# Moving the low weight buffers 128 bytes against the high ones in a two-block float32 encoder kernel

## The chip, the cores and the metric

The kernel runs on one NeuronCore of a Trainium2 chip. The metric is the device time of one execution in microseconds (us); the number of record is the median of several runs. Beside it there is one profiled execution, whose trace the rows below come from.

## The reference

Two encoder blocks in float32, on a sequence of 256 tokens (272 with 16 meta tokens) of width 1024, each two layers deep. Cut to what matters:

```python
# first block: layer 0 (even) is two attentions side by side, layer 1 (odd) a gated recurrence
zp = einsum('btd,de->bte', rms_norm(h, g), w_in)      # 1024 -> 4288 (even), 4096 (odd)
y = concat([mla_mixer(...), swa_mixer(...)]) * silu(gate)      # even
y = (lru_direction(forward) + lru_direction(reverse)) * silu(gate)   # odd
h = h + einsum('bte,ed->btd', y, w_out)               # 2048 -> 1024
# second block, two layers
for l in range(2):
    x = x + 0.5 * swiglu(rmsnorm(x), w_gate, w_up, w_down)     # ffn1: 1024 -> 2 x 2816 -> 1024
    x = x + hybrid_mixer(rmsnorm(x), ...)                      # pooling and a chunked linear attention
    x = x + 0.5 * swiglu(rmsnorm(x), ...)                      # ffn2
```

Nearly all arithmetic is in these matrix products; the four swiglu layers hold the largest part.

## The kernel before

**Three matmuls for one product.** The products have to keep float32 accuracy, so each operand is held as two parts: a high part (`hi` for weights, names that end in `h` for activations) and a low part, the remainder (`lo`, and names that end in `l`). Each weight piece comes from HBM into a buffer `raw`; ScalarE (ACT) writes `hi` from it and VectorE (DVE) writes `lo = raw - hi` (`cut`). `prod` then issues three matmuls for each block of 128 rows of the contraction: `hi` with the activation's high part, `hi` with its low part, and `lo` with its high part. The weights are the stationary operand (128 columns, 512 bytes of each partition), loaded into TensorE by an LDWEIGHTS that the profile lists as PEld; the activations are the moving operand, of 256 columns in most stages and 272 in the first block:

```python
self.mm(out=out, lhsT=hi if i < 2 else lo, rhs=(xl if i == 1 else xh)[:, k, cols], ...)
```

**What stands where.** Four `hi` and four `lo` buffers of 4096 bytes for each partition lie one after the other in the pool `const` (`make`); a fifth pair is added by `more_cuts` after the even layer. `xh` and `xl` hold the normed activations; for 256 columns they are used through the views `sh` and `sl`, which `place` puts `X_AT` = 32 columns (128 bytes) behind the start of the tiles. `ph` and `pl` hold the hidden layer of a swiglu (22 blocks of 256 columns), `oyh`/`oyl`, `hh`/`hl`, `hph`/`hpl` and `mh`/`ml` the moving operands of the odd and the hybrid layers. `gap` takes some bytes of a pool so that what is allocated next starts later. A block of weights is 512 bytes and a block of 256 columns 1024 bytes, so all blocks of such a tile start at one residue modulo 256.

**Order.** The order of instructions is written by the program itself: `Builder` keeps a clock of assumed costs and lets helper routines run when their inputs are due. The order depends on these costs and on which buffer comes free first, not on addresses.

**Stages in the profile's time.** Even layer to about 309 us, odd layer to 455; then for each of the two layers of the second block: `ffn1` (gate and up products with `xh`/`xl`, then the down products with `ph`/`pl`), the hybrid layer, `ffn2`. The down products run at about 579 to 634, 922 to 992, 1108 to 1170 and 1466 to 1527 us. Counted in the code, one swiglu issues 22 x 2 x 8 x 3 = 1056 matmuls for gate and up and 8 x 22 x 3 = 528 for down.

Of the kernel before, what the change touches and what calls it, by code (L numbers as in the profile page):

```python
# [9 lines left out]
F32 = mybir.dt.float32  # L10
F32R = mybir.dt.float32r
# [5 lines left out]
P = 128  # L17
D = 1024
NM = 16
S = 256  # L20
T = NM + S
KD = D // P
# [40 lines left out]
def weight_plan():  # L63

    out = []

    def add(name, i, n, step=1024):
        out.append((name, i, [(a, min(a + step, n)) for a in range(0, n, step)]))

    for c in range(2):  # L70
        add("first", c, 2048)
    for c in range(2, 8):
        add("ein", c, 2048)
    add("evs", 0, 2048)
    for c in range(12, 16):
        add("ein", c, 2048)
    for c in range(3):
        add("uq", c, 1536, 768)
    for c in range(2):
        add("ukv", c, 2048)  # L80
    for c in range(8, 12):
        add("ein", c, 2048)
    for d in range(KD):
        add("eout", d, 2048)
    for kind, g in odd_order():
        if kind == "w":
            add("oout", g, 2048)
        else:
            for c in range(2):
                add("oin", 2 * g + c + 8 * (kind == "g"), 2048)  # L90
    for l in range(2):
        for f in ("ffn1", "ffn2"):
            for e in range(KFF):
                add(f + "_gu", l * KFF + e, 2048)
            for d in range(2 * KD):
                add(f + "_dn", l * 2 * KD + d, DFF // 2, 768)
            if f == "ffn1":
                for c in range(4):
                    add("hin", l * 16 + c, 2048)
                for c in range(2):  # L100
                    add("hi", l * 2 + c, 2048)
                for c in HYBRID:
                    add("hin", l * 16 + c, 2048)
                for c in range(4):
                    add("wph", l * 4 + c, 2048)
                for c in range(4):
                    add("hout", l * 4 + c, 2048)
    return out
# [11 lines left out]
class Clock:  # L120
# [4 lines left out]
    def __init__(self):  # L125
        self.at = dict.fromkeys(("pe", "act", "dve", "pool", "dma", "dma2"), 0.0)
        self.wrote, self.read = {}, {}
        self.mark, self.tables, self.banks = 0.0, (), set()

    def range(self, ap):  # L130
        dims = list(ap.ap)
        per = dims[0][0] or 1 << 30
        lo = ap.offset % per
        return ap.tensor.name, lo, lo + 1 + sum((n - 1) * abs(s) for s, n in dims[1:])
# [92 lines left out]
class Builder:  # L227

    AHEAD = 3
    X_AT = 32  # L230
    gaps = 0

    def __init__(self, ctx, tc, a):
        self.clock = Clock()
        self.ctx, self.tc, self.nc, self.a = ctx, tc, Core(tc.nc, self.clock), a
        nc = self.nc
        self.tt, self.ts, self.stt, self.ttr = nc.vector.tensor_tensor, nc.vector.tensor_scalar, nc.vector.scalar_tensor_tensor, nc.vector.tensor_tensor_reduce
        self.act, self.mm = nc.scalar.activation, nc.tensor.matmul
        self.cos, self.done, self.cur, self.lists, self.home, self.stalls = [], {}, None, {}, {}, 0
        self.loads = weight_plan()  # L240
        self.plan = [(n, i, ps, p) for n, i, ps in self.loads for p in range(len(ps))]
        self.load_at = self.conv_at = self.use_at = 0
        self.raws, self.conv = [], {}
        self.const = self.pool(ctx, "const")
        self.res = self.pool(ctx, "res", 2)
        psum = self.pool(ctx, "psum", space=PSUM)
        self.make(psum, "acc", 2, [P, 512])
        self.make(psum, "m", 6, [P, 512])
        self.make(self.const, "raw", 2, [P, 2048])
        self.make(self.const, "hi", 4, [P, 1024], F32R)  # L250
        self.make(self.const, "lo", 4, [P, 1024], F32R)
        self.make(self.const, "work", 8, [P, T + 4])
        self.make(self.const, "mx", 6, [P, 16])
# [9 lines left out]

    def gap(self, pool, n):

        if n:
            self.gaps += 1
            pool.tile([P, n // 4], F32, tag=f"gap{self.gaps}", name=f"gap{self.gaps}")

    def make(self, pool, name, n, shape, dt=F32):  # L270

# [221 lines left out]

    def feed(self, gen, d, x, g, n):
        if n == S:
            self.place(gen)
            self.split(x, self.sh[:, d, :], self.sl[:, d, :], g)
        else:
            self.split(x, self.xh[:, d, :n], self.xl[:, d, :n], g)
        self.put("x", gen, d)  # L500
        self.spawn(self.square(gen, d, x, n))

    def place(self, gen):

        at = self.X_AT
        self.sh, self.sl = [t.rearrange("p k t -> p (k t)")[:, at:at + KD * S].rearrange("p (k t) -> p k t", t=S) for t in (self.xh, self.xl)]

    def square(self, gen, d, x, n):
        yield from self.idle("act")
# [591 lines left out]
    def odd(self):  # L1101
# [5 lines left out]
        od = self.pool(st, "od")  # L1107
# [9 lines left out]
        n = 32  # L1117
        at = V_AT["lam"][0]
# [6 lines left out]
        def decay_rates():  # L1125
# [20 lines left out]
            ts(out=c8[:, 1, :], in0=r(5), scalar1=-8.0, scalar2=None, op0=ALU.mult)  # L1146
            self.put("c8")

        yh = [self.t(od, [P, G, S], f"oyh{i}", F32R) for i in range(2)]
        yl = [self.t(od, [P, G, S], f"oyl{i}", F32R) for i in range(2)]  # L1150
        xcs, zgs = {}, {}
# [277 lines left out]
    def more_cuts(self):  # L1429

        late = self.pool(self.ctx, "late")
        for n in ("hi", "lo"):
            self.lists[n].append(self.t(late, [P, 1024], n + "4", F32R))
        self.AHEAD = 4
        self.lbw = self.t(late, [P, 10, 4], "lbw")
        self.hyb = self.t(late, [P, H_N], "hyb")
        self.nc.sync.dma_start(out=self.hyb, in_=self.a["hyb"])
# [33 lines left out]
    def hybrid(self, layer, gen):  # L1471
# [5 lines left out]
        st = ExitStack()  # L1477
        self.phase(gen)
        hy = self.pool(st, "hy")
        self.gap(hy, 32)  # L1480
        self.make(hy, "kq", 2, [P, H, S])
        x, xh, xl = self.x, self.sh, self.sl
        cols = slice(0, S)
# [260 lines left out]
        for c in HYBRID:  # L1744
            e = 2 * c
            if e < 12:
                dst, name, e0 = up_, "u", 8
            elif e < 16:
                dst, name, e0 = og, "g", 12
                self.need("og free", gen)  # L1750
            else:
                dst, name, e0 = gz, "z", 16
# [257 lines left out]
```

## Time and profile before

| | |
|---|---|
| median of 3 runs | 1540.03 us (1538.16 to 1541.54) |
| profiled execution, its own time | 1542.62 us |
| its span, first to last instruction | 1540.5 us |
| TensorE (PE) busy | 1507.8 us, 98%, 12950 matmuls |
| weight loads (PEld) busy | 1473.7 us, 96% |
| DVE busy, ACT busy | 1115.9 us (72%), 904.9 us (59%) |
| mean granted TensorE clock | 0.996 |

How to read it: matmuls are pipelined, one starts before the one ahead of it has ended, so the busy share says that TensorE is always at work, but not how fast. The pace is read from the time between the starts of two matmuls, or from how many of them a stretch holds. A matmul's record lasts about 0.28 us, so a count over a stretch takes in some 2.4 that began before it.

### The profile page before, as it was taken

Reading aid. Unit: us, or ns where it says so; the run is one execution under the profiler, and the core shown is the slowest. Engines: PE = TensorE matmul, PEld = TensorE weight load, DVE = VectorE, ACT = ScalarE, POOL = GpSimd, SP = SyncE. Lnnn points to the kernel's source line nnn. Section 1 sums busy time; section 2 is a strip of 40 time slices with the busy share of each in tenths; the row PEclk is TensorE's granted clock in tenths of the full one; section 3 lists DMA queues with packets and bytes.
Section 4 is the critical chain, followed back from the end, with each engine's and each line's share of the span. In section 5 each row is a group of like instructions: output and inputs, shape, how many; then the busy total and the mean of one; then the engine's idle time right before and its main releaser. Section 6 shows DMA issues by size and latency. Waiting matters only on the chain.

```text
span 1540.5 us, 31049 instructions
## 1 busy us (share of the span) xinstructions
PE 1507.8 (98%) x12950; PEld 1473.7 (96%) x12950; DVE 1115.9 (72%) x1882; ACT 904.9 (59%) x1435; POOL 26.2 (2%) x68
## 2 busy tenths in 40 slices
PE   8999999999989999999999999999999998999998
PEld 8989899999989999989999999999999998999998
DVE  6977775689996666668886666666666787777754
ACT  7666654699966545475455544455455754555453
POOL 1000000000000000000000000000000000000000
PEclk9999999999999999999999999999999999999999
DMA  6422224554445645644355555556456433456553
GB/s 240 152 90 83 84 81 164 182 174 143 156 174 189 218 167 183 211 161 165 137 195 189 196 177 174 194 194 214 161 188 209 167 138 137 163 189 222 175 174 117
DMA packets 42492, 259.12 MB, mean 168 GB/s; under 512 B 4840, under 2 KB 6256, under 8 KB 18416
## 3 DMA queue, kind: packets, MB, share of 16 engines
q1 hardware_dynamic: 40624, 251.90, 47.1%
q10 hardware_dynamic: 1728, 5.24, 1.0%
q8 instruction: 101, 1.65, 0.4%
q14 instruction: 39, 0.32, 0.1%
HBM read 256.07 MB, written 1.05 MB: 167 GB/s over the span
## 4 chain that ended last, share of the span: by engine, by line
PE 63%; issue 19%; DVE 10%; ACT 5%; DMA 2%; POOL 0%; POOLq 0%; ACTq 0%; SPq 0%; DVEq 0%
PE acc L181 51%; PE m L181 12%; DVE lo L181 4%; DVE big L181 3%; ACT hi L181 2%; DMA raw<-in_hin_dram 1%; ACT L181 1%; DVE kq L181 1%; ACT big L181 1%; ACT w L181 0%; DVE xc L181 0%; ACT xx L181 0%; DVE xx L181 0%; DMA raw<-in_ffn_gu_dram 0%; DVE work L181 0%
## 5 line engine op out<-in xcount | busy, mean ns | idle before, releaser
L181 DVE TENSOR_TENSOR lo<-raw,hi 128x1024 fp32r<-128x1024 f32 (+3 forms) x520 | 582.7, 1129 | 258.5 <-ACT hi L181 254.8
L181 ACT ACTIVATE hi<-raw 128x1024 fp32r<-128x1024 f32 (+3 forms) x520 | 502.2, 980 | 297.0 <-PE acc L181 207.8
L181 PE MATMUL acc<-xh,hi 128*128 128x256 f32 (+1 forms) x2096 | 589.7, 281 | 5.4 <-ACT hi L181 5.4
L181 PE MATMUL acc<-xl,hi 128*128 128x256 f32 (+1 forms) x2096 | 590.5, 282 | 0.0
L181 PE MATMUL acc<-xh,lo 128*128 128x256 f32 (+1 forms) x2096 | 588.7, 281 | 0.1
L181 PEld LDWEIGHTS acc<-xh,hi 128*128 128x128 f32 x2096 | 394.5, 188 | 6.8 <-ACT hi L181 5.4
L181 PEld LDWEIGHTS acc<-xl,hi 128*128 128x128 f32 x2096 | 395.6, 189 | 1.4
L181 PEld LDWEIGHTS acc<-xh,lo 128*128 128x128 f32 x2096 | 394.6, 188 | 1.6 <-DVE lo L181 0.5
L181 PE MATMUL acc<-pl,hi 128*128 128x256 f32 x704 | 196.9, 280 | 0.0
L181 PE MATMUL acc<-ph,lo 128*128 128x256 f32 x704 | 196.6, 279 | 0.0
L181 PE MATMUL acc<-ph,hi 128*128 128x256 f32 x704 | 196.4, 279 | 0.0
L181 PEld LDWEIGHTS acc<-pl,hi 128*128 128x128 f32 x704 | 132.2, 188 | 0.0
L181 PEld LDWEIGHTS acc<-ph,hi 128*128 128x128 f32 x704 | 132.2, 188 | 0.0
L181 PEld LDWEIGHTS acc<-ph,lo 128*128 128x128 f32 x704 | 131.8, 187 | 0.0
L181 PE MATMUL m<-xh,lo 128*128 128x256 f32 (+1 forms) x336 | 96.0, 286 | 0.0
L181 PE MATMUL m<-xl,hi 128*128 128x256 f32 (+1 forms) x336 | 95.6, 284 | 0.0
L181 PE MATMUL m<-xh,hi 128*128 128x256 f32 (+1 forms) x336 | 95.5, 284 | 0.0
L181 DVE TENSOR_TENSOR work<-acc,spread 128x256 f32<-128x256 f32 (+1 forms) x108 | 46.0, 426 | 38.0 <-PE acc L181 35.3
L181 ACT ACTIVATE work<-work 128x256 f32<-128x256 f32 (+2 forms) x92 | 37.4, 408 | 51.9 <-DVE work L181 51.5
L181 PEld LDWEIGHTS m<-xh,lo 128*128 128x128 f32 x336 | 63.6, 189 | 0.3
L181 PEld LDWEIGHTS m<-xh,hi 128*128 128x128 f32 x336 | 63.6, 189 | 0.2
L181 PEld LDWEIGHTS m<-xl,hi 128*128 128x128 f32 x336 | 63.5, 189 | 0.1
(359 smaller groups left out, 2242.4 us busy)
## 6 DMA issues: line engine op xcount, KB each, us to landing
raw<-in_ffn_gu_dram SPq DMA_DIRECT2D x88, 1024.0 KB, 4.9
raw<-in_ffn_dn_dram SPq DMA_DIRECT2D x64, 704.0 KB, 4.1
raw<-in_hin_dram SPq DMA_DIRECT2D x32, 1024.0 KB, 4.9
raw<-in_oin_dram SPq DMA_DIRECT2D x16, 1024.0 KB, 5.0
raw<-in_ein_dram SPq DMA_DIRECT2D x12, 1024.0 KB, 4.7
raw<-in_eout_dram SPq DMA_DIRECT2D x8, 1024.0 KB, 4.9
raw<-in_oout_dram SPq DMA_DIRECT2D x8, 1024.0 KB, 4.9
raw<-in_wph_dram SPq DMA_DIRECT2D x8, 1024.0 KB, 4.9
```

What stands on the lines that cost most here:

```text
L181: r = f(*args, **kw)
```

## The change

No instruction is added, removed or moved: on each of the five engines the built program has the same instructions with the same operands in the same order as before. What changes is the address at which tiles start. In the built programs, in bytes modulo 256:

| tile | before | after |
|---|---|---|
| `hi0` to `hi4` | 128 | 128 |
| `lo0` to `lo4` | 128 | 0 |
| `sh`, `sl` (`xh`, `xl` for 256 columns) | 64 | 64 |
| `ph`, `pl` | 192 | 64 |
| `oyh`, `oyl`, `hh`, `hl`, `hph`, `hpl`, `mh`, `ml` | 64 | 64 |
| `xh`, `xl` for 272 columns, block k | 192 + 64 k | 64 + 64 k |

`sh` and `sl` keep the very addresses they had: the tiles start 128 bytes later and the offset of 32 columns inside them is gone. `ff` keeps its gap of 160, so `ph` and `pl` shift with what lies below them.

```diff
@@ class Builder @@
     AHEAD = 3
-    X_AT = 32
     gaps = 0
...
         self.make(self.const, "hi", 4, [P, 1024], F32R)
+        self.gap(self.const, 128)
         self.make(self.const, "lo", 4, [P, 1024], F32R)
...
-    def place(self, gen):
-
-        at = self.X_AT
-        self.sh, self.sl = [t.rearrange("p k t -> p (k t)")[:, at:at + KD * S].rearrange("p (k t) -> p k t", t=S) for t in (self.xh, self.xl)]
+    def place(self):
+
+        self.sh, self.sl = [t.rearrange("p k t -> p (k t)")[:, :KD * S].rearrange("p (k t) -> p k t", t=S) for t in (self.xh, self.xl)]
...
@@ odd @@
+        self.gap(od, 128)
         yh = [self.t(od, [P, G, S], f"oyh{i}", F32R) for i in range(2)]
...
@@ more_cuts @@
-        for n in ("hi", "lo"):
-            self.lists[n].append(self.t(late, [P, 1024], n + "4", F32R))
+        self.gap(late, 128)
+        self.lists["hi"].append(self.t(late, [P, 1024], "hi4", F32R))
+        self.gap(late, 128)
+        self.lists["lo"].append(self.t(late, [P, 1024], "lo4", F32R))
...
@@ hybrid @@
-        self.gap(hy, 32)
+        self.gap(hy, 160)
         self.make(hy, "kq", 2, [P, H, S])
```

## Rows read from the trace of the kernel before

**Rows 1.** The page: busy time by engine, and the granted TensorE clock by slice.
```profile
PE 1507.8 (98%) x12950; PEld 1473.7 (96%) x12950; DVE 1115.9 (72%) x1882; ACT 904.9 (59%) x1435; POOL 26.2 (2%) x68
...
PEclk9999999999999999999999999999999999999999
```
**Rows 2.** What TensorE waited for, the longest total: us, times, longest.
```profile
PE m L181 <- DVE kq L181: 6.4, 12, 0.9
```
**Rows 3.** TensorE groups by form: shape, count, busy us, mean ns, idle before.
```profile
L181 PE MATMUL acc<-xl,hi 128*128 128x256 f32 x1816 | 506.0, 279 | 0.0
...
L181 PE MATMUL acc<-pl,hi 128*128 128x256 f32 x704 | 196.9, 280 | 0.0
...
L181 PE MATMUL acc<-xl,hi 128*128 128x272 f32 x280 | 84.4, 302 | 0.0
...
L181 PE MATMUL m<-xl,hi 128*128 128x256 f32 x232 | 64.7, 279 | 0.0
```
**Rows 4.** Busy time by stretch of the span, all engines.
```profile
core 0: us, PE busy (x) PEld busy (x) DVE busy (x) ACT busy (x) POOL busy (x), PEclk, DMA share, GB/s
470.00:570.00 100.00, 100.00 (x885) 100.00 (x884) 70.75 (x117) 62.39 (x89) 0.00 (x0) 1.00 0.57 201
...
812.00:918.00 106.00, 105.23 (x892) 104.83 (x891) 69.86 (x105) 55.13 (x80) 1.61 (x1) 1.00 0.53 186
...
1000.00:1104.00 104.00, 104.00 (x920) 104.00 (x919) 69.11 (x100) 55.39 (x81) 0.00 (x0) 1.00 0.56 193
...
1304.00:1345.00 41.00, 41.00 (x342) 41.00 (x342) 29.85 (x56) 21.48 (x35) 0.00 (x0) 0.97 0.41 139
...
580.00:634.00 54.00, 54.00 (x461) 54.00 (x460) 34.48 (x55) 26.22 (x40) 0.00 (x0) 1.00 0.55 183
929.00:991.00 62.00, 62.00 (x529) 62.00 (x528) 39.27 (x61) 31.76 (x48) 0.00 (x0) 1.00 0.55 187
```
**Rows 5.** TensorE groups by form, 475 to 565 us, then 812 to 912 us.
```profile
L181 PE MATMUL acc<-xl,hi 128*128 128x256 f32 x248 | 68.4, 276 | 0.0
...
L181 PE MATMUL acc<-xl,hi 128*128 128x256 f32 x256 | 72.1, 282 | 0.0
```
**Rows 6.** Timeline where `ffn1` goes from gate/up to down: start, length (us).
```profile
578.36 0.28 PE L181 MATMUL acc<-xh,hi 128*128 128x256 f32 x1
...
578.70 0.28 PE L181 MATMUL acc<-ph,hi 128*128 128x256 f32 x1
...
579.05 0.28 PE L181 MATMUL acc<-ph,hi 128*128 128x256 f32 x1
...
579.41 0.28 PE L181 MATMUL acc<-ph,hi 128*128 128x256 f32 x1
```
**Rows 7.** Timeline where `ffn2` down ends and the next `ffn1` begins.
```profile
991.54 0.28 PE L181 MATMUL acc<-ph,hi 128*128 128x256 f32 x1
...
991.90 0.28 PE L181 MATMUL acc<-xh,hi 128*128 128x256 f32 x1
...
992.25 0.28 PE L181 MATMUL acc<-xh,hi 128*128 128x256 f32 x1
```
**Rows 8.** Timeline of the odd layer's gate products, first and last of 13.
```profile
344.71 0.28 PE L181 MATMUL m<-xh,hi 128*128 128x256 f32 x1
...
346.12 0.28 PE L181 MATMUL m<-xh,hi 128*128 128x256 f32 x1
```
**Rows 9.** Timeline of a matmul, and of the weight load that starts with it.
```profile
499.94 0.28 PE L181 MATMUL m<-xl,hi 128*128 128x256 f32 x1
...
499.94 0.19 PEld L181 LDWEIGHTS m<-xh,lo 128*128 128x128 f32 x1
```
**Rows 10.** VectorE groups, the costliest: the making of `lo`.
```profile
L181 DVE TENSOR_TENSOR lo<-raw,hi 128x1024 fp32r<-128x1024 f32 (+3 forms) x520 | 582.7, 1129 | 258.5 <-ACT hi L181 254.8 <-PE acc L181 1.5 <-PE m L181 1.4
```

More of the change, by code (lines that the diff above doesn't have):

```diff
@@ L264, in gap @@
     def gap(self, pool, n):
-        if n:
-            self.gaps += 1
-            pool.tile([P, n // 4], F32, tag=f"gap{self.gaps}", name=f"gap{self.gaps}")
+        self.gaps += 1
+        pool.tile([P, n // 4], F32, tag=f"gap{self.gaps}", name=f"gap{self.gaps}")
     def make(self, pool, name, n, shape, dt=F32):
@@ L495, in feed @@
         if n == S:
-            self.place(gen)
+            self.place()
             self.split(x, self.sh[:, d, :], self.sl[:, d, :], g)
```

## The prediction

> **What bounds the kernel now.** I read the page first: TensorE is busy 98% of the span, at the full granted clock in every slice [rows 1]. The waits come next, to see whether another engine holds it up: the longest total is 6.4 us [rows 2], so speeding up or slowing down DVE, ACT or the DMA queues by a little ends nowhere. The time is the number of matmuls times the time from one start to the next, and the change can act on that spacing alone, since it moves no instruction. The groups show that three shapes of three matmuls (high-high, high-low, low-high) carry the kernel, 256 columns each, 1816, 704 and 232 times for each of the three, and that 272 columns come to far less [rows 3]. With the smaller groups there are some 9360 matmuls of 256 columns.
>
> The stretches then give the spacing. From 470 to 570 us TensorE starts 885 matmuls less the 2.4 that lap in: 100 us / 882.6 = 113.3 ns. The same stage one layer on gives 104 / 917.6 = 113.3 ns. From 812 to 918 us, the same program text on `ffn2`, it is 105.2 / 889.6 = 118.3 ns, a little high because eight small matmuls are among them. The two stretches of down products give 54 / 458.6 = 117.7 and 62 / 526.6 = 117.7 ns, and the end of the second hybrid layer 41 / 339.6 = 120.7, where the count also pays for a short stretch at the lower clock [rows 4]. So there are two spacings, 113.3 and close to 117.8 ns; call them fast and slow; the record of one matmul shows them as well, 276 ns against 282 [rows 5]. No wait stands behind the slow one: idle before these groups is 0.0.
>
> Where do they change? At the turn from gate/up to down the start-to-start time of three goes from 0.34 us to 0.35 and 0.36 at once [rows 6]: the moving operand goes from residue 64 to 192 there, the weights staying at 128. The four down stages are all slow. In the other direction, from `ph` back to `xh`, three matmuls still take 0.35 us [rows 7]. So with the moving operand at 64 both spacings can last for a whole stage, and which one it is depends on what came before; at 192 only the slow one is seen. A third piece: in the odd layer's gate products the moving operand of 256 columns goes 0, 64, 128, 192 from one block to the next, and twelve matmuls take 1.41 us, 117.5 ns each, with no fast stretch in between [rows 8]. The weights for a matmul are loaded while the one ahead of it runs: the load of a `lo` block begins with the matmul that uses `xl` [rows 9]. What decides is then, as far as these rows go, where the weights being loaded start against the moving operand being read: 128 - 64 = +64 bytes allows the fast spacing, 128 - 192 = -64 does not.
>
> [...]
>
> **The change, part by part.**
>
> *Low weights at 0.* After the change two loads of three (`hi`) stand at 128 - 64 = +64 against the moving operand and one (`lo`) at 0 - 64 = -64, everywhere. The lower bound of the cost: only the matmul under which `lo` is loaded becomes slow, (2 x 113.3 + 117.8) / 3 = 114.8 ns. The upper bound: a relation that changes within each three leaves no fast stretch at all, as in the gate products, 117.8 ns. I take a value two thirds of the way up, 114.8 + 2/3 x 3.0 = 116.8 ns, because the rows nearest to it (a relation that changes all the time) are slow throughout, and because one step with -64 was enough to end a fast stretch at the turn to `ph`.
>
> *Whom it touches.* Fast before: gate and up of both `ffn1` and of the last `ffn2`, 3 x 1056 = 3168; the end of the first hybrid layer, 384. Slow: gate and up of the first `ffn2`, 1056; the end of the second hybrid layer, 384; the down products, 4 x 528 = 2112. That leaves some 2260 in the odd layer and in the two hybrid layers, where both spacings occur; I halve them. So 4680 fast, 2570 slow at 64 and 2112 slow at 192; the mean is 115.5 ns.
>
> *Moving operands at one residue.* `sh` and `sl` stay where they are, and `oyh`, `hh`, `hph` and `mh` keep their residue: nothing. `ph` and `pl` go from -64 to the mixed relation of all others and so take its 116.8 ns.
>
> *The sum.* 4680 x (116.8 - 113.3) = +16.4 us; 2570 x (116.8 - 117.8) = -2.6; 2112 x (116.8 - 117.7) = -1.9. Together +11.9 us.
>
> *272 columns.* The residues of the moving operand only start at another place of the same circle of four; `lo` changes its relation in one load of three. Spacing is 126 ns or so there and depends on the block; a third of the difference found above, 1.5 ns, over some 1600 matmuls bounds it at 2.4 us either way. I take 0, between them.
>
> *VectorE, ScalarE, DMA.* The writes of `lo` go to other addresses; one takes 1129 ns on DVE, which is busy 71 of 100 us in the fastest stage [rows 4, 10]. Even if it slowed by a tenth, it would lie behind TensorE. The gaps themselves cost a few hundred bytes of SBUF and no instruction. Cost nothing.
>
> The profiled execution took 1542.6 us, span 1540.5, and is 2.6 above the median. 1542.6 + 11.9 = 1554.5 for such an execution, and 1540.0 + 11.9 = **1552 us** for the median.
>
> **The rivals.** All by the new spacing s of 256 columns, each as a mean over the stages; the sign turns at s = 115.5 ns, the mean before.
>
> - *All slow:* s = 117.8. 4680 x 4.5 = +21 us: 1561. For it: the gate products, and the slow stretch that lasts from `ph` into `xh`. Against it: two loads of three keep +64.
> - *Each load by itself:* s = 114.8 everywhere. +7.0 - 7.7 - 6.1 = -7 us: 1533. For it: that is what "the relation of this load decides" would say. Against it: at +64 the slow spacing also lasts, for 106 us at a time.
> - *Fast everywhere (the other side):* a low weight half a period away breaks up the slow order, which then cannot last, and the three find a steady order at 113.3. It saves 2570 x 4.5 + 2112 x 4.4 = 21 us: 1519. For it: both orders are kept up by history, so a shift can just as well remove the slow one; `ph` comes to 64. Against it: no row with a relation that changes is fast.
> - *Nothing:* s stays as it is stage by stage, history decides alone: 1540. Against it: the down products are slow in all four stages.
>
> **How the numbers follow.** Chances: slow with a part kept (my forecast) 0.32, all slow 0.20, nothing 0.13, each load by itself 0.13, fast everywhere 0.22. Faster by over 0.2% (about what a measurement of this kernel can tell from no change) is the sum of the last two, 0.35; slower 0.52; within it 0.13. The likeliest case alone reaches from 1545 to 1559. Since both signs hold much, the range goes from fast everywhere less the bound of the 272 columns, 1517, to all slow plus the same, 1563.
>
> **What would show it.** The same stretches of the profile after: gate and up of `ffn1` at 276 ns and 113.3 ns before should come out near 280 ns and 116 to 118, in every layer alike and without stages of two kinds; the down products between 115 and 118. If the down products come out at 113.3 and no stage at 117.8, the step from "the relation of `lo` is that of `ph`" to "so it is slow" is wrong. If `ffn1` stays fast, one load of three does not break the order. DVE and DMA rows should not move. A spacing below 113.3 anywhere would mean that what I take for the fast order is itself a partly blocked one, and the gain could then pass my range.

## The result: 12 us faster, where 12 us slower was forecast

The changed kernel took 1529.33 us (median of 5 runs, 1526.28 to 1529.65) against 1541.54 us (median of 5 runs of the kernel before on the same chip, 1538.16 to 1546.21). The ratio is 0.991, 95% interval 0.989 to 0.994. The time lies inside the forecast range, but on the other side of no change: the range took in every rival, so that it held the result is no merit of the forecast; to being faster the prediction gave 0.35. The profiled execution of the changed kernel took 1526.28 us, 16.3 us less than the one that [rows 1 to 10] come from.

The page of the changed kernel, busy time by engine and the granted clock, answers to [rows 1]. TensorE issues the same 12950 matmuls in 15 us less; the other engines and the clock did not move.

```profile
PE 1492.8 (98%) x12950; PEld 1458.6 (96%) x12950; DVE 1116.3 (73%) x1882; ACT 903.1 (59%) x1435; POOL 26.2 (2%) x68
...
PEclk9999999999999999999999999999999999999999
```

TensorE groups of the changed kernel by form (shape, count, busy us, mean ns, idle before) answer to [rows 3]: the down products with `pl` went from 280 to 276 ns for one record, and 276 was the mark of the fast spacing in [rows 5]. The 272-column group did not gain.

```profile
L181 PE MATMUL acc<-xl,hi 128*128 128x256 f32 x1816 | 504.3, 278 | 0.0
...
L181 PE MATMUL acc<-pl,hi 128*128 128x256 f32 x704 | 194.3, 276 | 0.0
...
L181 PE MATMUL acc<-xl,hi 128*128 128x272 f32 x280 | 84.7, 303 | 0.0
```

Stretches of the changed kernel, columns as in [rows 4]: gate and up of the first `ffn1`, its down products, gate and up of the first `ffn2`, its down products, and the end of the second hybrid layer.

```profile
470.00:570.00 100.00, 100.00 (x885) 100.00 (x884) 70.34 (x117) 62.65 (x88) 0.00 (x0) 1.00 0.57 198
580.00:630.00 50.00, 50.00 (x444) 50.00 (x443) 33.41 (x52) 25.53 (x41) 0.00 (x0) 1.00 0.56 183
810.00:916.00 106.00, 105.77 (x934) 105.57 (x933) 71.73 (x106) 57.22 (x83) 1.61 (x1) 1.00 0.55 193
926.00:984.00 58.00, 58.00 (x515) 58.00 (x514) 37.58 (x58) 29.32 (x44) 0.00 (x0) 1.00 0.57 194
...
1292.00:1333.00 41.00, 41.00 (x354) 41.00 (x354) 30.45 (x58) 23.08 (x36) 0.00 (x0) 0.97 0.43 147
```

Less the 2.4 that lap in, that is 100/882.6 = 113.3 ns, 50/441.6 = 113.2, 105.77/931.6 = 113.5, 58/512.6 = 113.1, and 41/351.6 = 116.6. The first stretch was fast before and stayed so; the other four were at 117.7 to 120.7 [rows 4]. At the turn from gate/up to `ph`, where three matmuls went from 0.34 to 0.35 and 0.36 us [rows 6], nothing happens now: three take 0.34 us, and the first two with `ph` 0.23 (timeline: start, length):

```profile
578.65 0.28 PE L181 MATMUL acc<-xh,hi 128*128 128x256 f32 x1
...
578.99 0.28 PE L181 MATMUL acc<-xh,hi 128*128 128x256 f32 x1
...
579.33 0.28 PE L181 MATMUL acc<-ph,hi 128*128 128x256 f32 x1
...
579.56 0.28 PE L181 MATMUL acc<-ph,lo 128*128 128x256 f32 x1
```

I also took the starts of the same-numbered matmuls in both traces, stage by stage. Before, the four down stages begin at 578.7, 929.7, 1112.8 and 1469.7 us and last 62.07 us each from first to last start; now each lasts 59.73. That is 2.34 us less for each, 9.4 together; gate and up of the first `ffn2` lost 5.1, the second hybrid layer 2.0, and every other stage, the two layers of the first block among them, moved by 0.5 us or less. All stages together come to 16.2 us, beside 16.3 between the two profiled executions: the gain lies in stages that were slow and became fast, and no stage that was fast became slow. What is still slow is mainly the odd layer's gate products, one record of 281 ns in the changed kernel (group by form, 345.5 to 347.5 us):

```profile
L181 PE MATMUL m<-xl,hi 128*128 128x256 f32 x6 | 1.7, 281 | 0.0
```

One thing in the trace before refines what the prediction read from it. Gate and up of the first `ffn2` did not start slow: 8/70.6 = 113.3 ns up to 812.5 us, after a hybrid layer that had ended fast, and 98/831.6 = 117.8 from 820 us on (columns as in [rows 4]).

```profile
804.50:812.50 8.00, 8.00 (x73) 8.00 (x72) 4.99 (x7) 2.95 (x5) 0.00 (x0) 1.00 0.64 245
...
820.00:918.00 98.00, 98.00 (x834) 98.00 (x834) 64.70 (x95) 52.17 (x77) 0.00 (x0) 1.00 0.55 197
```

Between the two TensorE waited once and issued four small matmuls; three matmuls took 0.33 us ahead of them and 0.35 behind:

```profile
812.70 0.28 PE L181 MATMUL m<-xh,hi 128*128 128x256 f32 x1
...
813.03 0.28 PE L181 MATMUL acc<-xh,hi 128*128 128x256 f32 x1
814.00 0.61 PE L181 MATMUL m<-cst,acc 128*128 128x1 f32 x4 [0.69 <-DVE acc L181]
...
814.79 0.28 PE L181 MATMUL m<-xh,hi 128*128 128x256 f32 x1
...
815.14 0.28 PE L181 MATMUL m<-xh,hi 128*128 128x256 f32 x1
```

The other way round, the second `ffn1` took over the slow spacing from the down products ahead of it and became fast behind four small matmuls at 1000.23 us: three took 0.35 to 0.36 us ahead of them and 0.34 from 1000.92 us on. So "what came before" is not only the stage ahead: at these two places the spacing switched at a short interruption, once in each direction. In the changed kernel the same small matmuls are issued, and behind them the spacing is 113.3 ns again (36 steps from 812.24 to 816.32 us).

### The profile page after: what moved, and what is told of

Read it like the earlier page. It is cut to its first block, busy times and chain, and to the rows that moved or that the text cites. A ratio compares the mean times of both kernels' runs of the same rounds, so it can differ in the third digit from the quotient of the medians.

```text
span 1524.5 us, 31049 instructions
## 1 busy us (share of the span) xinstructions
PE 1492.8 (98%) x12950; PEld 1458.6 (96%) x12950; DVE 1116.3 (73%) x1882; ACT 903.1 (59%) x1435; POOL 26.2 (2%) x68
## 4 chain that ended last, share of the span: by engine, by line
PE 60%; issue 26%; DVE 8%; ACT 4%; DMA 1%; POOL 1%; SPq 0%; ACTq 0%; DVEq 0%; POOLq 0%
PE acc L181 45%; PE m L181 14%; DVE lo L181 3%; ACT hi L181 2%; DVE big L181 2%; DVE kq L181 1%; ACT w L181 1%; ACT L181 1%; ACT xx L181 1%; DVE xx L181 0%; DVE lf L181 0%; DVE work L181 0%; DMA raw<-in_hin_dram 0%; DMA raw<-in_hi_dram 0%; POOL col L181 0%
## 5 line engine op out<-in xcount | busy, mean ns | idle before, releaser
L181 DVE TENSOR_TENSOR lo<-raw,hi 128x1024 fp32r<-128x1024 f32 (+3 forms) x520 | 582.6, 1129 | 248.0 <-ACT hi L181 243.6
```

The lines of the kernel that those rows point to most:

```text
L181: r = f(*args, **kw)
```

## The experiments

Three kernels take the change apart in the model, timed beside the kernel before (1541.64 us, 24 runs, 1536.42 to 1546.14). Two kernels leave the model out and time the threes of matmuls alone, with all other engines idle in the stretches read; each of the two ran once.

### lo_only: the low weights alone

```diff
         self.make(self.const, "hi", 4, [P, 1024], F32R)
+        self.gap(self.const, 128)
         self.make(self.const, "lo", 4, [P, 1024], F32R)
+        self.gap(self.const, 128)
...
-        for n in ("hi", "lo"):
-            self.lists[n].append(self.t(late, [P, 1024], n + "4", F32R))
+        self.lists["hi"].append(self.t(late, [P, 1024], "hi4", F32R))
+        self.gap(late, 128)
+        self.lists["lo"].append(self.t(late, [P, 1024], "lo4", F32R))
+        self.gap(late, 128)
```

The second gap of each pair leaves all that follows at its residue of before (`X_AT` stays 32). Expected:

> The low weights alone go to residue 0; ph stays at 192, everything else at its residue of before. Theory A (weights half a period of 256 bytes apart break up the slow order, wherever the moving operand stands): all stages of 256 columns at 113.3 ns, the down products at ph = 192 too, as in the changed kernel, about 1529 us. Theory B (a moving operand 64 bytes below the high weights is needed as well): the down products stay at 117.8 ns, which is 2112 x 4.5 ns = 9.5 us more than the changed kernel, about 1539 us; gate and up of the first ffn2 become fast.

Measured 1538.29 us (12 runs, 1536.41 to 1541.39), ratio 0.998 (0.997 to 1.000). The same stretches in its trace: first `ffn1`, its down products, first `ffn2`.

```profile
470.00:570.00 100.00, 100.00 (x884) 100.00 (x884) 70.30 (x118) 62.35 (x89) 0.00 (x0) 1.00 0.59 202
580.00:630.00 50.00, 50.00 (x423) 50.00 (x423) 31.46 (x50) 25.05 (x39) 0.00 (x0) 1.00 0.54 175
812.00:916.00 104.00, 102.56 (x902) 102.16 (x901) 71.20 (x107) 55.95 (x81) 1.61 (x1) 1.00 0.55 190
```

Gate and up of `ffn2` became fast, 102.56/899.6 = 114.0 ns with its small matmuls in it. The down products, `ph` at 192, stayed slow, and at 50/420.6 = 118.9 ns a little slower than before. Theory A falls; B stands here: with `lo` at 0 the stages with the moving operand at 64 are fast and those at 192 are not.

### ph_only: the hidden layer alone

```diff
-        self.gap(ff, 160)
+        self.gap(ff, 32)
```

> ph and pl alone go from residue 192 to 64; low and high weights both stay at 128. Theory A (the weights' distance decides): with equal residues both orders can last, so the down products go on with whatever spacing the gate and up products ended with; gate and up of the first ffn2 stay at 117.8 ns. Between 1532 us (three down stages of four fast, 3 x 528 x 4.5 ns = 7 us) and 1541 us. Theory B (the moving operand's residue decides): all four down stages at 113.3 ns and 9.5 us less than before, about 1531 us.

Measured 1537.15 us (12 runs, 1529.47 to 1542.69), ratio 0.997 (0.996 to 0.999). Down products of the first `ffn1`, gate and up of the first `ffn2`, its down products:

```profile
580.00:630.00 50.00, 50.00 (x444) 50.00 (x443) 33.44 (x52) 25.30 (x41) 0.00 (x0) 1.00 0.55 181
812.00:916.00 104.00, 102.94 (x872) 102.54 (x871) 68.54 (x102) 54.00 (x78) 1.61 (x1) 1.00 0.55 190
930.00:988.00 58.00, 58.00 (x495) 58.00 (x494) 37.09 (x59) 29.47 (x45) 0.00 (x0) 1.00 0.57 192
```

The first down stage goes on fast at 113.2 ns after a fast gate/up stage; in `ffn2` gate and up run at 118.4 and its down products at 58/492.6 = 117.7, though nothing about their addresses differs. By the starts of their matmuls three of the four down stages became fast; the third holds 443 from 1110 to 1160 us, 50/440.6 = 113.5 ns. So with both weights at 128 and the moving operand at 64 both orders last, as A says of this set; the residue of `ph` alone does not settle it, and B in its pure form falls. The times tell the same: 13.2 us between fastest and slowest of 12 runs, against 5.0 us in the 12 of `lo_only` and 3.4 us in the 5 of the changed kernel. By itself `lo` brings 3.4 us in the medians and `ph` 4.5; the changed kernel, which has both, brings 12.2, more than their sum.

### swap: the residues of hi and lo exchanged

The changed kernel with `hi` at 0 and `lo` at 128, the rest where it was.

```diff
+        self.gap(self.const, 128)
         self.make(self.const, "hi", 4, [P, 1024], F32R)
         self.gap(self.const, 128)
         self.make(self.const, "lo", 4, [P, 1024], F32R)
+        self.gap(self.const, 128)
...
-        self.gap(late, 128)
         self.lists["hi"].append(self.t(late, [P, 1024], "hi4", F32R))
         self.gap(late, 128)
         self.lists["lo"].append(self.t(late, [P, 1024], "lo4", F32R))
+        self.gap(late, 128)
```

> The changed kernel with the residues of the two weights exchanged: hi at 0, lo at 128, so that two loads of three stand 64 bytes below the moving operand and one 64 above. Theory A (only the distance between the weights counts): no stage slow, about 1529 us. Theory C (two loads of three at +64 are what keeps the fast order): the slow order wins everywhere, 4439 - 558 = 3881 steps of 117.8 instead of 113.3 ns back and the rest too, 1545 to 1561 us.

Measured 1551.79 us (7 runs, 1543.69 to 1557.70), ratio 1.007 (1.004 to 1.009) against the kernel before. First `ffn1` and its down products, then the second `ffn1` and its down products:

```profile
475.00:575.00 100.00, 100.00 (x844) 100.00 (x843) 66.20 (x110) 59.16 (x83) 0.00 (x0) 1.00 0.56 194
586.00:636.00 50.00, 50.00 (x423) 50.00 (x422) 31.46 (x50) 25.08 (x39) 0.00 (x0) 1.00 0.53 178
...
1010.00:1110.00 100.00, 100.00 (x884) 100.00 (x884) 67.31 (x96) 53.52 (x78) 0.00 (x0) 1.00 0.57 197
1122.00:1172.00 50.00, 50.00 (x444) 50.00 (x443) 32.26 (x50) 25.02 (x40) 0.00 (x0) 1.00 0.55 181
```

100/841.6 = 118.8 and 50/420.6 = 118.9 ns, then 113.4 and 113.2 for the same text one layer on. The distance between the weights is that of the changed kernel, so A falls once more. C is right that which weight stands above the moving operand matters, but not that the slow order wins everywhere: this set of residues is two-valued too, with 118.9 in place of 117.8 as its slow value.

### micro: a table of residues

For `hi` at 128, the weights `lo` and the moving operand at four residues each. `hc` is `hi`; `la`, `lb`, `lc`, `ld` stand at 0, 64, 128, 192, and so do `xa` to `xd` (high part of the moving operand) and `ya` to `yd` (low part). The loop, shortened (the pauses are copies on ScalarE):

```python
for l in "cdab":
    for r in "abcd":
        triples(fresh, l, r, 80)      # after a pause
        triples(lead, "c", "d", 32)   # lo at 128, moving at 192
        triples(after, l, r, 80)
```

In the built program the first eight matmuls of `after` mostly stand ahead of the lead, which waits; the rest (232 of 240 in 11 of the 16 cells) follow the lead without a gap, the first lead ending at 49.61 + 11.58 = 61.19 us and they beginning at 61.19, and they are what is read below.

> A kernel of its own that leaves the model out: for each of four residues of the low weights (128, 192, 0, 64; the high weights at 128) and four of the moving operand (0, 64, 128, 192) it issues 80 threes of matmuls of 256 columns twice: once after a pause (fresh), once straight after 32 threes with low weights at 128 and moving operand at 192 (lead, then after). Theory A: low weights at 128: slow order 117.8 ns at moving 192 always, and at 64 after the lead, fast at 64 after a pause; low weights at 0: 113.3 ns in all eight cells of fresh and after. Theory B: low weights at 0 fast only at moving 64. Theory C does not forbid A or B here. Low weights at 192 and 64, a quarter of the period, have no row yet: A as it stands gives between 113.3 and 117.8.

Stretches of 20 us inside five cells: `lo` 128 with moving 64, fresh and after; `lo` 0 with moving 64, fresh and after; `lo` 0 with moving 192, fresh. There is no DVE column, since it does nothing, and no DMA to speak of.

```profile
core 0: us, PE busy (x) PEld busy (x) ACT busy (x) POOL busy (x), PEclk, DMA share, GB/s
92.00:112.00 20.00, 20.00 (x179) 20.00 (x178) 0.00 (x0) 0.00 (x0) 1.00 0.00 1
132.00:152.00 20.00, 20.00 (x172) 20.00 (x172) 0.00 (x0) 0.00 (x0) 1.00 0.01 2
...
650.00:670.00 20.00, 20.00 (x179) 20.00 (x178) 0.00 (x0) 0.00 (x0) 1.00 0.01 2
690.00:710.00 20.00, 20.00 (x179) 20.00 (x178) 0.00 (x0) 0.00 (x0) 1.00 0.01 2
...
788.00:808.00 20.00, 20.00 (x170) 20.00 (x169) 0.00 (x0) 0.00 (x0) 1.00 0.00 1
```

20/176.6 = 113.3 and 20/169.6 = 117.9 for one and the same set; 113.3 and 113.3; 119.3 (one matmul more or less in the count is 0.7). More closely, from the starts of the last 61 matmuls of each cell (their distance / 60), in ns, one number where fresh and after agree to 0.1:

| | moving 0 | moving 64 | moving 128 | moving 192 |
|---|---|---|---|---|
| `lo` 128 | 118.7 | 113.3 fresh, 117.8 after | 120.0 | 117.8 |
| `lo` 192 | 120.0 | 118.2 | 117.8 | 117.8 |
| `lo` 0 | 118.3 | **113.3** | 119.1 | 118.9 |
| `lo` 64 | 120.0 fresh, 117.8 after | 117.8 | 117.8 | 115.6 |

One cell of sixteen is fast both times, `lo` 0 with moving 64: of its run after the lead, the first seven gaps behind the lead are 115 to 122 ns, and then the fast order stands. It is the one into which the change puts all operands of 256 columns outside the odd layer's gate products. The kernel before had its two kinds of stages in the first row: the two-valued cell for moving 64, and a cell that is slow in every reading for `ph`. `lo_only` moves `ph` to the last cell of the third row, 118.9, which its trace shows; B as it stood in the expectation describes the row of `lo` at 0 in this run. Two readings do not show that a cell has one value only: `micro2` has 113.3 for `lo` 0 with moving 192. For the cell of the change more readings speak: its runs and leads in `micro2` and the stages of 256 columns in the changed kernel.

### micro2: pairing, order, 272 columns, and the other lead

```python
CELLS = [(hxl("hc", l, r, r), 272, SLOW) for l in ("lc", "la") for r in "abcd"]
CELLS += [(hxl("hc", l, r, q), 256, SLOW) for l in ("lc", "la") for r, q in ("bd", "db")]
CELLS += [(hxh("hc", "l" + l, r, r), 256, SLOW) for l, r in ("cb", "ab", "ad")]
CELLS += [(hxl("hc", l, r, r), 256, SLOW) for l in ("lc", "la") for r in ("ab", "bc")]
CELLS += [(hxl("hc", "lc", "b", "b"), 256, FAST), (hxl("hc", "la", "d", "d"), 256, FAST), (hxl("la", "lc", "b", "b"), 256, FAST)]
```

`hxl` is the kernel's order, `hxh` issues the two products with the high activations first; `SLOW` is the lead of `micro`, `FAST` is `lo` 0 with moving 64. The two letters in quotes are the high and the low part's tile; `xab` and `xbc` stand at 32 and 96.

> Again threes of matmuls without the model, hi at 128: 50 threes fresh, then 24 threes of a lead, then the same 50 after. Theory P (what counts is, for each load, where the weights being loaded stand against the moving operand read at that moment): with lo left at 128 and only the low activations moved to 192 (xh at 64), the load of lo stands at -64 and the other two at +64, as in the changed kernel, so 113.3 ns fresh and after the slow lead; with lo at 0, xh at 64 and xl at 192 all loads stand at +64, so 113.3 fresh and 117.8 after, as in the kernel before; the order hi-high, lo-high, hi-low at lo 0, moving 64 gives 113.3 in both. Theory Q (the addresses of the two weights against each other count, not the pairing in time): the first of these stays two-valued (113.3 fresh, 117.8 after) and the second is 113.3 in both. After a fast lead: lo 128, moving 64 stays 113.3; lo 0, moving 192 is 118.9 if no fast order exists there and 113.3 if one does; hi 0, lo 128, moving 64 must read the same as the last one if relations alone count. 272 columns at one residue in all blocks: 272/256 x 113.3 = 120.4 ns where 256 columns are fast, 125 or more elsewhere. Moving operands at 32 and 96: between 113.3 and 120.0, no theory says which.

Stretches of 13 us: `lo` 128 with the high part at 64 and the low part at 192, fresh; `lo` 0 with both at 192, fresh, and after the fast lead; `hi` 0, `lo` 128, both at 64, fresh, and after the fast lead; `hxh` with `lo` 0 and moving 64, after the slow lead; 272 columns, `lo` 128, moving 64, fresh.

```profile
416.00:429.00 13.00, 13.00 (x113) 13.00 (x112) 0.00 (x0) 0.00 (x0) 1.00 0.01 1
...
969.00:982.00 13.00, 13.00 (x117) 13.00 (x116) 0.00 (x0) 0.00 (x0) 1.00 0.00 1
996.00:1009.00 13.00, 13.00 (x112) 13.00 (x111) 0.00 (x0) 0.00 (x0) 1.00 0.00 1
1015.00:1028.00 13.00, 13.00 (x111) 13.00 (x111) 0.00 (x0) 0.00 (x0) 1.00 0.01 1
1042.00:1055.00 13.00, 13.00 (x117) 13.00 (x116) 0.00 (x0) 0.00 (x0) 1.00 0.00 1
...
676.00:689.00 13.00, 13.00 (x117) 13.00 (x116) 0.00 (x0) 0.00 (x0) 1.00 0.00 1
...
77.00:90.00 13.00, 13.00 (x108) 13.00 (x107) 0.00 (x0) 0.00 (x0) 1.00 0.01 1
```

A count of 117 is 13/114.6 = 113.4 ns, 111 to 113 are 119.7 to 117.5. By starts 60 apart:

- High part at 64, low part at 192, `lo` 128: 117.8 fresh and after. Theory P falls: load by load the distances are those of the changed kernel (+64, -64, +64), and it is slow. With `lo` 0 the same pair gives 120.9, where both P and Q have 113.3 fresh. Theory Q, which had the first of these two-valued and the second at 113.3 both times, falls too. High at 192, low at 64: 117.8 everywhere.
- `lo` 0 with moving 192 is two-valued: 113.3 fresh here (118.9 fresh in `micro`), 118.9 after either lead. `hi` 0, `lo` 128, moving 64, which has the same distances modulo 256: 118.9 fresh, 113.3 after the fast lead. That is the set of `swap`, and it shows its two kinds of stages without the model. The two sets have the same two values, but after one and the same fast lead the first reads 118.9 and the second 113.3; they were to read the same if distances alone count. For sets with two values that leaves it open. What a pause leaves is open too: the run ahead of the fresh one with `lo` 0, moving 192 was slow in `micro` (119.1) and fast in `micro2` (113.3).
- After the fast lead `lo` 128 with moving 64 stays at 113.3, after the slow one it takes 117.8.
- The order `hxh` changes nothing at moving 64: `lo` 128 is two-valued, `lo` 0 at 113.3 both times.
- Moving operands at 32 and 96: 117.3 to 118.4. In none of the eight readings does the fast spacing show, 32 bytes away from the residue that has it.
- 272 columns: 123.3 at `lo` 128, moving 64; 124.4 to 126.7 in the seven others. No cell reaches 120.4.

No kernel of these beats the changed one. Giving the odd layer's gate products one residue as well would need rows of 320 columns, 3 KB more of each partition for `xh` and `xl` together; it wasn't tried.

## Why the prediction was wrong, point by point

- *What bounds the kernel* was right: TensorE's spacing, and nothing else. The result came from the spacing alone; VectorE's `lo` writes took 1129 ns before and after, so "cost nothing" held for them. That the clock was full "in every slice" is read a little too far, a 9 on the page standing for 90% or more: the end of the second hybrid layer is at 0.97 [rows 4], and at 0.97 after the change as well.
- *Two spacings, kept up by history* was right for the set of addresses that the prediction read it from. `micro` shows both in that set with every other engine idle, and `ph_only` flips between them from stage to stage. As a list of what occurs it was too short: other residues have spacings from 115.6 to 120.9 ns, and history includes short interruptions, as at 814 us above.
- *The failed step* is the inference from "the relation of `lo` is that of `ph`" to "so it is slow", which set s = 116.8 ns; the trace after has 113.1 to 113.5 ns in gate/up and down, with `lo` at 0 and the moving operand at 64. I took the gate products as the nearest row, because their relation changes all the time, and the turn to `ph`, because one step with -64 ended a fast stretch. Neither has the case of the change in it. In the gate products the moving operand stands at 0, 128 or 192 for three blocks of four, cells that are slow in the table or can be (118.3, 119.1, 118.9 for `lo` 0; 118.7, 120.0, 117.8 for `lo` 128); at the turn to `ph` the relation of all three loads changes at once. Neither shows what a `lo` at 0, beside a `hi` at 128, does while the moving operand stays at 64: 113.3 ns. That the down products come out at 113.3 and no stage at 117.8 was the sign that the prediction had named for this step being wrong; in the second block it is what came.
- *The variable was wrong beneath it.* I argued with the distance of each load from the moving operand. `micro2` has two sets with the same distances load by load, at 113.3 and 117.8 ns. What the runs show as deciding is the set of residues of all four parts (high and low weights, high and low activations), together with what ran before where the set is two-valued. Residues were taken modulo 256 throughout, and no run tests that period by itself.
- *The rival "fast everywhere"*, with a chance of 0.22, had the direction, and its reason holds for the set that the change makes: with `hi` at 128, `lo` at 0 and the moving operand at 64 the slow order did not last. `micro` shows it directly, 113.3 ns seven gaps after a lead at 117.8. As a rule on weights 128 bytes apart modulo 256 the reason fails: the down products of `lo_only` are at 118.9 ns and stages of `swap` at 118.8. Against it I held that no row with a relation that changes is fast; such rows were all at other moving residues.
- *Its size*, 21 us, was too large, and by one term. The down products were put at 2112 x 4.4 = 9.3 us and gave 9.4; gate and up of `ffn2` and the end of the second hybrid layer at 1440 x 4.5 = 6.5 and gave 7.1. The remaining 1130 of the halved 2260 were to give 5.1 and gave nothing: counted where the mean over twelve starts is above 116 ns, only some 640 of these matmuls were slow before, 460 of them in the odd layer, where some 390, mainly the gate products, are slow after the change as well. So 16.3 in the profiled pair. The medians differ by 12.2, since the profiled execution of the kernel before is 1.1 us above its median and that of the changed kernel, its fastest, 3.1 below its own.
- *The rival "nothing"* is out, and so is "each load by itself", which had 114.8 ns for the stages that came out at 113.3. The addresses were worth 12.2 us in the medians, and in the two kernels of threes alone the spacing goes from 113.3 to 120.9 ns with the residues and with what ran before.
- *272 columns* at nothing was right: from the first matmul to number 2150, which takes in the even layer and 1500 of the 1692 matmuls of the threes with 272 columns, it was 314.40 us before and 314.52 after.

What stays open is the part of the chip in which such an order arises. The runs show where it is, and that no other engine is needed for it; not why 32 bytes matter, nor why the one set showed no lasting slow order.

## What to carry to other kernels

When a stage that only TensorE bounds shows two spacings for one shape, put the start addresses of the operands beside them, and measure a table of residues with the threes alone before arguing from distances: here one run of that kind settled what the inference had wrong. Look for a set that is fast after a slow lead, not only after a pause, and read it more than twice; a two-valued set can show itself in the scatter of the whole kernel (13 us in `ph_only` and 14 in `swap`, against 3 in the changed kernel). And before a row is taken as the nearest, check that it differs from the case in one thing only.

## Not expected

- One shape of 256 columns has spacings of 113.3, 115.6, 117.3, 117.8, 118.2 to 119.1, 120.0 and 120.9 ns in `micro` and `micro2`, by residues and, where a set is two-valued, by what ran before, at a granted clock of 1.00 with VectorE idle and next to no DMA traffic.
- Within such an order the spacing holds: the means over the last 60, 120 and 180 gaps of a cell of `micro` agree to 0.1 ns. After a pause with TensorE idle for 0.97 us in `micro` and 0.98 in `micro2` the same residues can come out in either order (`lo` 0, moving 192: 118.9 in `micro`, 113.3 in `micro2`).
- 272 columns at the best set cost 123.3 ns, 9% more than 113.3 for 6% more columns.
